# Delta-rule encoder layer: inverse merges in chunk order, and whole stationaries for the learned tokens

## Chip, core and metric

One core of a Trainium2 chip. The metric is the device time of one execution in microseconds; three executions of the kernel before took 2045.39, 2044.15 and 2043.72 us, median 2044.15. All arithmetic is in float32.

## What is computed

One layer of a bidirectional encoder on 1024 tokens, ahead of which 16 learned tokens are put. The part that matters here is the gated delta rule of branch A, for 8 heads in both directions. Cut from the reference (the kernel uses its own chunk size, 128):

```python
kk = jnp.einsum("bnhid,bnhjd->bnhij", k, k)
lmat = jnp.where(strict, beta[..., :, None] * kk * decay, 0.0)
a = lmat + jnp.eye(CHUNK, dtype=lmat.dtype)
rhs = jnp.concatenate([v * beta[..., None], k * (beta * jnp.exp(g))[..., None]], axis=-1)
sol = lax.linalg.triangular_solve(a, rhs, left_side=True, lower=True, unit_diagonal=True)
u, w = sol[..., :dv], sol[..., dv:]
...
def step(S, inp):
    v_new = u_c - jnp.einsum("bhcd,bhde->bhce", w_c, S)
    o_c = (jnp.einsum("bhcd,bhde->bhce", qd_c, S)
           + jnp.einsum("bhij,bhje->bhie", qk_c, v_new))
    S = S * gl_c[..., None, None] + jnp.einsum("bhcd,bhce->bhde", kd_c, v_new)
```

Around it: RMSNorm and one input projection (1024 to 9248 columns), short convolutions, branch B, a merge with gates, and a SwiGLU of width 2816.

## The kernel before

**Stages.** After the norm of the input (up to about 60 us) comes the stage of the input projection, whose end in the trace lies near 1060 us; then branch outputs, merge and SwiGLU, which the change does not touch. In the projection stage each unit of 128 columns is a run of three-fold matmuls (L293, L294, L295: high by high, high by low, low by high halves of a split float32), in groups of 320 to 512 tokens.

**Order of the work.** Nothing is scheduled by the hardware or by a library there: the kernel is written as generators, one for each step of a head (`g_decay`, `g_norm`, `g_inv`, `g_scan`), and a planner with a clock of its own for each engine (`T`) runs them. After every projection step the planner lets those generators go on whose due time has come; each `yield` hands back the next due time, worked out from estimates such as `pe(215)` (add 215 ns to TensorE's clock). So the numbers in `pe(...)` decide between which projection matmuls a head's step stands in TensorE's queue. VectorE's long jobs, convolution (L316 to L324) and the forward substitution (L448, L452), are fed in by `pump` from the same clocks.

**The inverse of a head.** The 1024 tokens are 8 chunks of 128 (`NC = 8`). For each chunk and direction the inverse of a triangular 128x128 matrix is needed (`NP`). `g_inv` makes the inverses of the four 32x32 blocks on the diagonal by forward substitution, which go through DRAM, and then merges: 32 to 64, and 64 to 128. `B(b)` is partitions or columns 32b to 32b+31.

- First merge, product 1 (L661 to L663): for each of four pairs (direction d, blocks a and b) and each chunk, one matmul with a 32x32 stationary `NP[B(a), c, d, B(b)]` and 32 moving columns of an inverse block (in `X64` or `Xe`), into `pt[B(b), c]`. That is 32 matmuls; all results lie in one PSUM bank. A 32x32 matmul uses a corner of the array: its rows are set by the partitions of its operands (a), its columns by those of its result (b).
- ScalarE negates the result into `T2` (L666).
- Product 2 (L670 to L674): the same four pairs and 8 chunks, into `pp[B(a), c]` with stationary `T2` (L672), and for the two pairs with `X64` also the transposed product into `px[B(b), c]` (L674): 48 matmuls, in two banks.
- Six copies, on ScalarE and VectorE by turns, put the results into `NP` and `X64` (L677 to L685); then the second merge with 64x64 blocks (L691 to L704) goes on, whose two matmuls for a chunk already stand behind one another.

In the trace a float32 matmul is two records (a transpose is one), and the stationary's load is a row of its own (PEld).

**The learned tokens.** The 16 learned tokens are a short ninth chunk (index 8). Its keys: a transpose with a 128x16 stationary (L515, a record of the helper's line L83) and k by k (L516). Its inverse, `Pm`, a 16x16 tile, is made on GpSimd and comes by DMA (L633 to L635). In the scan: the transpose of vT (L724), then L738 (stationary `Pm`, 16x16), L741 on VectorE, L743 (stationary 16x128 of the keys `kn`), whose result is the first state S0 of the forward direction.

## Time and profile before

| what | value |
|---|---|
| median of three executions | 2044.15 us |
| span of the profiled execution | 2041.3 us |
| TensorE busy in it | 2003.0 us (98%) |
| VectorE, ScalarE, GpSimd busy | 1412.3, 790.9, 109.1 us |
| L663 records in all | 512 (64 for each head) |
| L672 and L674 records in all | 512 and 256 |
| L738 and L743 records in all | 16 and 16 |

The span runs from the first instruction to the last; what an execution takes beyond it lies around it and is not in the profile. A row of the timeline has a start, a length, the engine, the line in the program, the operation, "result<-operands", the shapes (for TensorE rows x columns of the stationary, then the moving shape) and a count where rows of one kind were put together; in brackets the idle time before it and who ended that. A matmul's length is its way through the array; matmuls overlap, so what a step costs is read from start to start.

### The profile page before, as it was taken

Reading aid. Unit: us, or ns where it says so; the run is one execution under the profiler, and the core shown is the slowest. Engines: PE = TensorE matmul, PEld = TensorE weight load, DVE = VectorE, ACT = ScalarE, POOL = GpSimd, SP = SyncE. Lnnn points to the kernel's source line nnn. Section 1 sums busy time; section 2 is a strip of 40 time slices with the busy share of each in tenths; the row PEclk is TensorE's granted clock in tenths of the full one; section 3 lists DMA queues with packets and bytes.
Section 4 is the critical chain, followed back from the end, with each engine's and each line's share of the span. In section 5 each row is a group of like instructions: output and inputs, shape, how many; then the busy total and the mean of one; then the engine's idle time right before and its main releaser. Section 6 shows DMA issues by size and latency. Waiting matters only on the chain.

```text
span 2041.3 us, 32116 instructions
## 1 busy us (share of the span) xinstructions
PE 2003.0 (98%) x12075; PEld 1745.0 (85%) x12075; DVE 1412.3 (69%) x3129; ACT 790.9 (39%) x1873; POOL 109.1 (5%) x392
## 2 busy tenths in 40 slices
PE   6999999999999999999999999999999999999998
PEld 6999899999999898978888888888888888888886
DVE  6789486887977686856445534458978778756576
ACT  5363235454544554453334211124323223224343
POOL 0002110202020020201000000000000000000000
PEclk9999999999999999999999999999999999999999
DMA  4122312222222213132326734122766355487654
GB/s 140 42 85 68 74 59 62 79 63 58 73 58 81 81 58 94 57 89 78 97 70 200 255 114 142 53 83 93 238 226 221 125 180 168 153 277 247 195 176 155
DMA packets 250722, 248.40 MB, mean 122 GB/s; under 512 B 46084, under 2 KB 190773, under 8 KB 248133
## 3 DMA queue, kind: packets, MB, share of 16 engines
q1 hardware_dynamic: 250565, 246.34, 38.6%
q8 instruction: 95, 1.56, 0.3%
q14 instruction: 62, 0.51, 0.1%
HBM read 179.62 MB, written 66.67 MB: 121 GB/s over the span
## 4 chain that ended last, share of the span: by engine, by line
PE 81%; DVE 11%; ACT 3%; DMA 1%; issue 1%; SPq 0%; ACTq 0%; DVEq 0%
PE pm L293 9%; PE pm L295 9%; PE pm L294 9%; PE pm L1335 3%; PE pm L1334 3%; PE pm L1333 3%; PE pd L1334 2%; PE pd L1335 2%; PE pd L1333 2%; DVE kq L316 2%; PE pe L1335 2%; PE pe L1334 2%; PE pe L1333 2%; PE pd L771 1%; PE pd L119 1%; PE pd L121 1%
## 5 line engine op out<-in xcount | busy, mean ns | idle before, releaser
L293 PE MATMUL pm<-hTh,wh 128*128 128x512 f32 (+4 forms) x1424 | 525.8, 369 | 2.0 <-ACT wh L896 1.0
L295 PE MATMUL pm<-hTh,wl 128*128 128x512 f32 (+4 forms) x1424 | 490.1, 344 | 0.2
L294 PE MATMUL pm<-al,wh 128*128 128x512 f32 (+4 forms) x1424 | 488.9, 343 | 0.3 <-DVE al L998 0.3
L293 PEld LDWEIGHTS pm<-hTh,wh 128*128 128x128 f32 x1424 | 268.4, 189 | 21.7 <-issue 2.7
L295 PEld LDWEIGHTS pm<-hTh,wl 128*128 128x128 f32 x1424 | 267.4, 188 | 20.9 <-DVE wl L893 1.2
L294 PEld LDWEIGHTS pm<-al,wh 128*128 128x128 f32 x1424 | 268.7, 189 | 15.4 <-DVE al L998 0.7
L87 DVE TENSOR_TENSOR al<-raw,ring_h 128x1024 fp32r<-128x1024 f32 x73 | 88.3, 1222 | 64.7 <-ACT ring_h L86 64.3
L893 DVE TENSOR_TENSOR wl<-raw,wh 128x512 fp32r<-128x512 f32 x134 | 90.5, 686 | 50.8 <-ACT wh L896 50.2
L86 ACT CAST ring_h<-raw 128x1024 fp32r<-128x1024 f32 x73 | 76.7, 1055 | 105.7 <-PE pe L1478 34.8
L316 DVE SCALAR_TENSOR_TENSOR kq<-ra,wc,kq 128x520 f32<-128x520 f32 x128 | 97.4, 761 | 5.3 <-ACT kq L346 3.9
L86 ACT CAST wh<-raw 128x1024 fp32r<-128x1024 f32 x45 | 47.4, 1053 | 123.0 <-issue 29.9
L896 ACT CAST wh<-raw 128x512 fp32r<-128x512 f32 x134 | 78.8, 618 | 9.7 <-PE pm L294 9.6
L778 ACT ACTIVATE w<-pd,small 128x128 f32<-128x128 f32 x128 | 40.0, 365 | 105.0 <-PE pd L771 85.7
L452 DVE TENSOR_TENSOR fP<-fP,tm 128x135 f32<-128x135 f32 (+23 forms) x248 | 72.2, 291 | 4.9
L448 DVE TENSOR_TENSOR tm<-fP,fN 128x135 f32<-128x135 f32 (+23 forms) x248 | 72.2, 291 | 4.2
L1337 DVE TENSOR_TENSOR b<-pm,b 128x512 f32<-128x512 f32 x67 | 45.1, 686 | 33.5 <-PE pm L1335 31.1
L800 DVE SCALAR_TENSOR_TENSOR S<-S,eGl,pd 128x128 f32<-128x128 f32 x104 | 31.8, 344 | 46.6 <-PE pd L788 29.4
L87 DVE TENSOR_TENSOR wl<-raw,wh 128x1024 fp32r<-128x1024 f32 x45 | 54.9, 1219 | 9.2 <-ACT wh L86 9.1
L617 POOL TENSOR_TENSOR tm<-mP,mN 1x15 f32<-1x15 f32 (+7 forms) x120 | 42.2, 352 | 274.2 <-DMA mN<-ndm 265.7
L1337 DVE TENSOR_TENSOR b<-pd,b 128x512 f32<-128x512 f32 x54 | 36.5, 686 | 22.2 <-PE pd L1335 22.2
L316 DVE SCALAR_TENSOR_TENSOR vT<-ra,wc,vT 128x520 f32<-128x520 f32 x64 | 48.3, 755 | 2.6 <-ACT vT L346 1.1
L486 ACT ACTIVATE PQ<-PQ,negG 128x128 f32<-128x128 f32 x128 | 43.2, 394 | 15.7 <-DVE PQ L481 15.6
(623 smaller groups left out, 4649.3 us busy)
## 6 DMA issues: line engine op xcount, KB each, us to landing
raw<-in_w_in_dram SPq DMA_DIRECT2D x72, 512.0 KB
raw<-in_w_gate_up_dram SPq DMA_DIRECT2D x44, 512.0 KB
sums<-in_w_down_dram SPq DMA_DIRECT2D x22, 512.0 KB
t_d<-sums SPq DMA_DIRECT2D x11, 1024.0 KB
raw<-s_d SPq DMA_DIRECT2D x44, 256.0 KB
raw<-t_d SPq DMA_DIRECT2D x44, 256.0 KB
act_d<-b SPq DMA_DIRECT2D x43, 256.0 KB
raw<-act_d SPq DMA_DIRECT2D x33, 256.0 KB
```

The costliest lines, as they stand in the source:

```text
L86: nc.scalar.copy(hi, src)
L87: nc.vector.tensor_tensor(out=lo, in0=src, in1=hi.bitcast(F32), op=ALU.subtract)
L293: mm(po[:, :n], wh[:, k], xh[:, k, t0:t0 + n], start=(k == 0), stop=False)
L294: mm(po[:, :n], wh[:, k], xl[k][:, t0:t0 + n], start=False, stop=False)
L295: mm(po[:, :n], wl[:, k], xh[:, k, t0:t0 + n], start=False, stop=(k == KT - 1))
L316: nc.vector.scalar_tensor_tensor(out=acc, in0=raw[:, h0 + t:h0 + t + hn], scalar=wc[:, t, col:col + 1], in1=acc, op0=ALU.mult, op1=ALU.add)
L893: nc.vector.tensor_tensor(out=u[1][1][:, k], in0=u[2][:, k], in1=u[1][0][:, k].bitcast(F32), op=ALU.subtract)
L896: nc.scalar.copy(u[1][0][:, k], u[2][:, k])
L1333: mm(po, ah[:, k], bhk, start=k == 0, stop=False)
L1334: mm(po, ah[:, k], blk, start=False, stop=False)
L1335: mm(po, al[:, k], bhk, start=False, stop=k == 3)
L1337: add = lambda out, a, b: nc.vector.tensor_tensor(out=out, in0=a, in1=b, op=ALU.add)
```

## The change

Three things are done.

1. Both products of the first merge are issued with the chunk as the outer loop and the four pairs behind one another, where the pair was the outer loop. The same 32 and 48 matmuls are there.
2. The learned tokens' chunk gets whole stationaries of 128x128: the keys' transpose and k by k take columns 0 to 127 (the 16 learned tokens and the next 112), the transpose of vT too; `Pm` becomes one of two tiles of 128x128 that are set to zero once on GpSimd and receive the 16x16 inverse in their corner, so that the other rows come out as zero; L738, L741 and L743 run over all 128 partitions.
3. The planner's estimates for these steps are set anew: 1150 for 4 x 300, 1600 for 4 x 450, 330 for 120.

```diff
@@ g_norm
-        transpose(pt[:META, :P], kT[:, 0:META])
-        mm(pt[:META, P:P + META], kT[:, 0:META], kT[:, 0:META], start=True, stop=True)
-        t = pe(120)
+        transpose(pt[:, :P], kT[:, 0:P])
+        mm(pt[:, P:P + META], kT[:, 0:P], kT[:, 0:META], start=True, stop=True)
+        t = pe(330)
...
-        nc.scalar.copy(kn[:META, 8], pt[:META, :P])
+        nc.scalar.copy(kn[:, 8], pt[:, :P])
@@ g_inv
-        Pm = dn.tile([META, META], F32, tag="Pm", name=uid("Pm"), bufs=2)
-        st_["Pm"] = Pm
-        nc.sync.dma_start(Pm, pdm)
+        Pm = st_["Pm"] = meta_inv[h % 2]
+        nc.sync.dma_start(Pm[:META, :META], pdm)
...
-        for d, a, b, Xs, xo in pairs:
-            for c in range(NC):
+        for c in range(NC):
+            for d, a, b, Xs, xo in pairs:
                 mm(pt[B(b), c], NP[B(a), c, d, B(b)], Xs[B(a), c, xo:xo + 32], start=True, stop=True)
-            pe(300)
-        yield T["pe"] + HOP
+        yield pe(1150)
...
-        for d, a, b, Xs, xo in pairs:
-            for c in range(NC):
+        for c in range(NC):
+            for d, a, b, Xs, xo in pairs:
                 mm(pp[B(a), c], T2[B(b), c], NP[B(b), c, d, B(b)], start=True, stop=True)
                 if Xs is X64:
                     mm(px[B(b), c], NP[B(b), c, d, B(b)], T2[B(b), c], start=True, stop=True)
-            pe(450)
-        yield T["pe"] + HOP
+        yield pe(1600)
@@ g_scan
-                if c == 8:
-                    transpose(pt[:META, i], vT[:, 0:META])
-                else:
-                    transpose(pt[:, i], vT[:, cs(c)])
+                transpose(pt[:, i], vT[:, 0:P] if c == 8 else vT[:, cs(c)])
...
-                p = META if c == 8 else P
-                nc.scalar.activation(vS[:p, c], pt[:p, i], AF.Copy, scale=sk[:p, c:c + 1])
+                nc.scalar.activation(vS[:, c], pt[:, i], AF.Copy, scale=sk[:, c:c + 1])
...
-        mm(bank[:META, 0], Pm, vS[:META, 8], start=True, stop=True)
+        mm(bank[:, 0], Pm, vS[:, 8], start=True, stop=True)
...
-        nc.vector.tensor_scalar(out=w[:META], in0=bank[:META, 0], scalar1=ce[:META, 8, 0:1], scalar2=None, op0=ALU.mult)
+        nc.vector.tensor_scalar(out=w, in0=bank[:, 0], scalar1=ce[:, 8, 0:1], scalar2=None, op0=ALU.mult)
...
-        mm(bank[:, 1], kn[:META, 8], w[:META], start=True, stop=True)
+        mm(bank[:, 1], kn[:, 8], w, start=True, stop=True)
@@ after the pool dn is opened
+    meta_inv = [dn.tile([P, P], F32, name=f"meta_inv{i}") for i in range(2)]
+    for m_ in meta_inv:
+        nc.gpsimd.memset(m_, 0.0)
```

How the instructions stand now. First TensorE's queue at product 1 of the first head (XT holds `X64`; a row is one call, x8 means eight alike), before:

```order
L295 MATMUL pm_2500<-hTh,wl_2393 128x322
L663 MATMUL pd_2524<-XT_2438,NP_1485 32x32 x8
L663 MATMUL pd_2524<-Xe_2437,NP_1485 32x32 x16
L663 MATMUL pd_2524<-XT_2438,NP_1485 32x32 x8
L293 MATMUL pm_2500<-hTh,wh_2392 128x322
```

and in the changed kernel (its line 662 is line 663 of before), the first five of its rows there:

```order
L295 MATMUL pm_2503<-hTh,wl_2397 128x322
L662 MATMUL pd_2527<-XT_2441,NP_1489 32x32
L662 MATMUL pd_2527<-Xe_2440,NP_1489 32x32 x2
L662 MATMUL pd_2527<-XT_2441,NP_1489 32x32 x2
L662 MATMUL pd_2527<-Xe_2440,NP_1489 32x32 x2
```

Eight matmuls on one corner followed one another before; now the corner changes with every matmul, and the four of a chunk are XT, Xe, Xe, XT.

Second, product 2 of the same head on TensorE (T is `T2`; line 672 of before is 670 now, 674 is 672), where before the pair with both results passes to the two pairs with one:

```order
L674 MATMUL pd_2570<-T_315_2523,NP_1485 32x32
L672 MATMUL pd_2569<-NP_1485,T_315_2523 32x32
L674 MATMUL pd_2570<-T_315_2523,NP_1485 32x32
L672 MATMUL pd_2569<-NP_1485,T_315_2523 32x32 x17
L674 MATMUL pd_2570<-T_315_2523,NP_1485 32x32
```

and now, the first chunk and the start of the second:

```order
L670 MATMUL pd_2572<-NP_1489,T_314_2526 32x32
L672 MATMUL pd_2573<-T_314_2526,NP_1489 32x32
L670 MATMUL pd_2572<-NP_1489,T_314_2526 32x32 x3
L672 MATMUL pd_2573<-T_314_2526,NP_1489 32x32
L670 MATMUL pd_2572<-NP_1489,T_314_2526 32x32
```

Each chunk now has all six of its matmuls behind one another.

Third, the start of the last head's scan on TensorE, from the last transposes of vT to the small matmul with the learned tokens' inverse, before:

```order
L83 MATMUL pd_12118<-ident,vT_9608 128x128 x3
L293 MATMUL pm_12083<-hTh,wh_11851 128x512
L294 MATMUL pm_12083<-al_122,wh_11851 128x512
L295 MATMUL pm_12083<-hTh,wl_11852 128x512
L293 MATMUL pm_12083<-hTh,wh_11851 128x512
L294 MATMUL pm_12083<-al_123,wh_11851 128x512
L295 MATMUL pm_12083<-hTh,wl_11852 128x512
L738 MATMUL pd_12133<-vS_12095,Pm_11839 16x128
```

and now (line 731):

```order
L83 MATMUL pd_12087<-ident,vT_9445 128x128 x3
L293 MATMUL pm_12034<-hTh,wh_11853 128x512
L294 MATMUL pm_12034<-al_123,wh_11853 128x512
L295 MATMUL pm_12034<-hTh,wl_11854 128x512
L731 MATMUL pd_12097<-vS_12066,meta_inv_657 128x128
```

The matmul's result has 128 rows where it had 16, and one projection step stands in between where there were two: the planner's changed clock has moved the step by one place.

## The prediction

> **What bounds the kernel now.** I read the windows by stage first, then the chain of waits, then TensorE's timeline at each place that the change touches. The change lies in the stage from 110 to 1060 us (projections with the delta rule's steps strewn in). Three windows, whose columns are the window, its length, busy time (x instructions) of PE, PEld, DVE, ACT, POOL, granted clock, DMA share and GB/s:

> ```profile
> 110.00:1060.00 950.00, 943.95 (x7150) 856.60 (x7149) 688.94 (x1956) 432.51 (x1365) 102.70 (x356) 1.00 0.26 73
> 110.00:200.00 90.00, 89.64 (x546) 85.68 (x545) 79.92 (x201) 45.91 (x160) 12.28 (x47) 1.00 0.28 80
> 1000.00:1060.00 60.00, 60.00 (x462) 50.25 (x461) 18.56 (x48) 22.80 (x64) 0.00 (x0) 1.00 0.23 67
> ```

> TensorE is idle for 6.05 of these 950 us, at full clock; the last window, with the last head's steps, has no idle TensorE at all, so no tail of waits hangs behind the last scan. VectorE has 261 us to spare over the stage, but at its start, up to 200 us, it is 89% busy. The chain that ended last says the same, and warns that VectorE is near:

> ```profile
> PE 81%; DVE 11%; ACT 3%; DMA 1%; issue 1%; SPq 0%; ACTq 0%; DVEq 0%
> ```

> So time that a step takes on TensorE's queue is time of the kernel, as long as the other engines keep up.

> **The change part by part.** Product 1 of the merge (L663) has 32 calls for each head; each call is two records in the trace, so 64 records. The first head's, columns start, length, engine, line, operation, count:

> ```profile
> 228.15 0.59 PE L663 MATMUL pd<-XT,NP 32*32 32x32 f32 x13
> 228.56 0.21 PE L663 MATMUL pd<-Xe,NP 32*32 32x32 f32 x1
> 228.59 0.19 PE L663 MATMUL pd<-XT,NP 32*32 32x32 f32 x1
> 228.61 0.19 PE L663 MATMUL pd<-Xe,NP 32*32 32x32 f32 x1
> ...
> 228.68 0.88 PE L663 MATMUL pd<-Xe,NP 32*32 32x32 f32 x26
> ...
> 229.49 0.57 PE L663 MATMUL pd<-XT,NP 32*32 32x32 f32 x13
> ```

> Read the last row first: 13 records of one pair in 0.57 us, the last of them 0.19 long, so twelve steps in 0.38 us: 0.0317 us from record to record as long as one pair stays on its own 32x32 corner of the array. Now the rows at 228.56: there the second pair (Xe) already runs while the first (XT) still ends, each at its own pace of about 0.03 us, and neither is slowed by the other. The first record starts at 228.15, the last at 229.49 + 0.57 - 0.19 = 229.87: 1.72 us, of which only these few overlaps at the three borders were saved. The new order puts the four pairs behind one another for each chunk, and all four lie on different corners (rows and columns 0,1; 2,3; 1,0; 3,2). If each keeps its pace, the stretch is that of one pair: 15 steps of 0.0317 = 0.48, with 0.02 for a slower first step and about 0.02 for the shifts between four starts, 0.52 us. Gain 1.20 us.

> Product 2 (L672 and L674, 48 calls, 96 records) already has places with two and with three corners at work:

> ```profile
> 231.53 0.21 PE L672 MATMUL pd<-NP,T 32*32 32x32 f32 x1
> 231.54 0.21 PE L674 MATMUL pd<-T,NP 32*32 32x32 f32 x1
> ...
> 231.99 0.19 PE L672 MATMUL pd<-NP,T 32*32 32x32 f32 x2
> 232.00 0.19 PE L674 MATMUL pd<-T,NP 32*32 32x32 f32 x1
> 232.03 0.19 PE L672 MATMUL pd<-NP,T 32*32 32x32 f32 x2
> 232.03 0.19 PE L674 MATMUL pd<-T,NP 32*32 32x32 f32 x1
> ...
> 233.26 0.19 PE L674 MATMUL pd<-T,NP 32*32 32x32 f32 x1
> ```

> At 231.99 to 232.03 three corners start a record each, and the next three follow about 0.03 us later: three cost what one does. (L672 and L674 of one pair share their rows of the array, so shared rows are no hindrance either.) The stretch is 231.53 to 233.26, 1.73 us. The new order has six corners in each chunk. With one pace for all it would be 0.52; but there are twelve records in each chunk, and neighbouring starts lie between 0.005 us (three from 231.99 to 232.00) and 0.01 us (231.53, 231.54) apart. I take 0.0065, nearer to the row with three corners: 8 x 12 x 0.0065 = 0.62 us; gain 1.11 us. Bounds for both products: at best the whole pace, 1.20 and 1.21; at worst what two corners show, 0.0317 / 2 for each record, which makes 1.01 and 1.52 us and a gain of 0.71 + 0.21.

> [...]

> Now the learned tokens. Two calls in the scan have stationaries of 16 rows (L738 also 16 columns); beside them a place with four records of full stationaries:

> ```profile
> 244.29 0.34 PE L294 MATMUL pm<-al,wh 128*128 128x384 f32 x1
> 244.46 0.34 PE L295 MATMUL pm<-hTh,wl 128*128 128x384 f32 x1
> 244.73 0.39 PE L738 MATMUL pd<-vS,Pm 16*16 16x128 f32 x2
> ...
> 245.39 0.40 PE L294 MATMUL pm<-al,wh 128*128 128x512 f32 x1
> ...
> 246.08 0.39 PE L294 MATMUL pm<-al,wh 128*128 128x512 f32 x1
> 246.31 0.39 PE L295 MATMUL pm<-hTh,wl 128*128 128x512 f32 x1
> 246.63 0.48 PE L743 MATMUL pd<-w,kn 16*128 16x128 f32 x2
> ...
> 247.38 0.40 PE L294 MATMUL pm<-al,wh 128*128 128x512 f32 x1
> ...
> 257.25 0.39 PE L295 MATMUL pm<-hTh,wl 128*128 128x512 f32 x1
> 257.48 0.61 PE L771 MATMUL pd<-r,NP 128*128 128x128 f32 x4
> ...
> 258.16 0.39 PE L294 MATMUL pm<-al,wh 128*128 128x512 f32 x1
> ```

> From the L295 ahead to the second projection matmul behind, less the steps of the two projections in between (0.17 for 384 columns, 0.23 for 512, both from start to start here): L738 costs 0.93 - 0.17 - 0.23 = 0.53 us, L743 1.07 - 0.46 = 0.61, and four full records 0.91 - 0.46 = 0.45, so two of them 0.22. The small shapes lose their time in front and behind, where the array passes from the full shape to the small one and back. With full stationaries L738 gains 0.31 and L743 0.39: 0.70 us for each head.

> The learned tokens' keys (L515 and L516, ahead of four full transposes):

> ```profile
> 116.10 0.31 PE L294 MATMUL pm<-al,wh 128*128 128x320 f32 x1
> 116.24 0.31 PE L295 MATMUL pm<-hTh,wl 128*128 128x320 f32 x1
> 116.39 0.27 PE L83 MATMUL pe<-ident,kq 128*16 128x128 f32 x1
> 116.59 0.21 PE L516 MATMUL pe<-kq 128*16 128x16 f32 x2
> 116.74 0.66 PE L83 MATMUL pe<-ident,kq 128*128 128x128 f32 x4
> ...
> 117.38 0.31 PE L294 MATMUL pm<-al,wh 128*128 128x320 f32 x1
> ```

> That is 1.14 - 2 x 0.15 = 0.84 us for seven records. Full stationaries with few moving columns are seen in the gates, where two records step by 0.23 although only 72 columns move:

> ```profile
> 100.78 0.39 PE L1120 MATMUL pe<-gc,Ub 128*128 128x72 f32 x2
> 101.01 0.39 PE L1120 MATMUL pe<-gc,Eb 128*128 128x72 f32 x2
> ```

> Seven records of 0.11 are 0.77: gain 0.07 us. Were L516's records as short as half of that, it would be 0.18; I keep 0.07. The short transpose of vT among two full ones I set at nothing: it moves the same 128 columns either way, and the short transpose at 116.39 starts one ordinary step of 0.15 behind its projection, so there is no gap to win in front of a transpose. The wider copies on ScalarE and VectorE (L520, L730, L741) cover 128 partitions with as many elements in each, so they cost what they did. The DMA of the inverse into the larger tile keeps its size and its place on SyncE's queue. The two memsets on GpSimd add a wait: they stand in its queue until the start-up tiles whose memory they take are free, and behind them stand the small memsets of the convolution's rows (L343), for which ScalarE's copies of the projections and the convolution wait.

> ```profile
> 68.82 0.10 POOL L343 MEMSET ra<- 128x2 f32 x1 [62.74 <-DVE kq L316]
> ```

> The first of those had itself to wait for VectorE until 68.82, after 62.74 us without work, so the new wait is covered if the start-up tiles are free by then; the price is nothing, or once a few microseconds in the convolutions.

> Sum for each head: 1.20 + 1.11 + 0.70 + 0.07 = 3.08 us, for eight heads 24.6 us, all on TensorE's queue.

> What is late next: the copies behind product 2.

> ```profile
> 233.48 0.36 ACT L682 COPY NP<-pd 32x256 f32<-32x256 f32 x1 [3.00 <-PE pd L674]
> ...
> 235.64 0.36 ACT L685 COPY XT<-pd 32x256 f32<-32x256 f32 x1 [0.94 <-DVE XT L684]
> ```

> They already begin when the last record of product 2 has ended (233.26 + 0.19), not pair by pair, so the new order takes nothing from them; they hand on to each other until 236.00, 2.7 us after that last record started, and the second half of the next merge waits for them where fewer projections lie between. The planner's counts have moved a little, so some heads have a projection step less there: I allow 0.8 us in all. VectorE gets 3 us less for each head in a stage where it has 261 to spare, and I allow 1.5 us for places where it is just in time. 24.6 - 2.3 = 22.3 us.

> The profiled execution's span is 2041.3 us, 2.85 under the median of 2044.15; the loss of 22.3 from the span goes one to one into the time: 2041.3 - 22.3 = 2019.0 us of span, and 2021.9 us.

> **The rivals.** Two at a time: the array or its queue serves no more than two corners in one pace. For it: the steady stretches in product 2 are of two; three are seen only over a few records. Gain (0.71 + 0.21 + 0.77) x 8 = 13.5 us, less 1 given back: 2031.6 us.

> One bank: pairs that write the same PSUM bank from different rows exclude each other as soon as they alternate, and the overlaps seen at the borders are an exception. Without overlap product 1 is 64 x 0.0317 = 2.03 us and the 64 records of L672 too, 0.31 and 0.30 worse than now; 0.77 - 0.61 = 0.16 us for each head remains, 1.3 us in all: 2042.9 us. Against it stand the rows at 228.56 and 232.03. [...]

> Slower: VectorE becomes the bound. The planner's costs are changed, so heads' steps are placed earlier among the projections, and TensorE comes sooner to results that VectorE has still to make. Its place is the key products, which wait already:

> ```profile
> PE pe L542 <- DVE PQ L571: 2.9, 5, 0.9
> ```

> (2.9 us in five waits, longest 0.9.) It decides once the waits grow by more than the 24.6 us won, over 3 us for each head, as if every one of the 64 L542 calls came some 0.45 us too early and not five of them. With 29 us of it the time is 2048.6. Against it: VectorE is 73% busy over the stage, and the 89% lie ahead of the first merge, where only the keys' 0.07 us are won; and the amount of projection work between the steps of a head is about the same in both orders.

> **How the numbers follow.** Forecast 0.70, between 2018 and 2027; two at a time 0.15, 2029 to 2034; VectorE taking back half of the gain 0.04, 2027 to 2040; one bank 0.07, 2040 to 2044; slower 0.04. The predicted time is the forecast's, 2021.9. At its lower end all records keep the pace (0.8 us more), L516 is shorter (0.9) and nothing is given back (2.3): 2017.9; I set 2017. The upper end takes in two at a time: 2034. A measurement of this kernel can tell 0.2%, 4.1 us, from no change. Faster by more than that: 0.70 + 0.15 + 0.04 and 0.02 of one bank, 0.91; within: 0.05; slower: 0.04.

> **What would show it.** In the changed kernel's timeline product 1 should take about 0.5 us from first to last start and product 2 about 0.6; 1.0 and 1.5 would be the rival with two; 2.0 each the bank. The scan's two small calls should stand as 128*128 with some 0.22 us of cost. TensorE's idle time from 110 us on should stay under 10 us, with L542 and the second merge at the head of what waits; 30 us there would be the slower rival. The forecast is wrong if the stretches are short and the time is still above 2034.

## The result and the profile after

The changed kernel takes 2034.13 us (median of four executions, 2032.91 to 2035.01), the kernel before 2044.77 us (2043.72 to 2046.32): a ratio of 0.9946 with a 95% interval of 0.9934 to 0.9959. It is 10.6 us faster where 22.3 were forecast, and lies just above the range's upper end, 2034. The profiled execution's span went from 2041.3 to 2031.6 us.

Two windows of the changed kernel (the columns as before), the first of them the one that the prediction began with:

```profile
110.00:1060.00 950.00, 934.81 (x7217) 853.41 (x7217) 696.88 (x1980) 439.01 (x1386) 101.20 (x356) 1.00 0.27 74
300.00:400.00 100.00, 95.82 (x802) 89.33 (x801) 73.68 (x206) 45.66 (x154) 11.79 (x44) 0.98 0.23 62
```

In the same 950 us TensorE now gets through 7217 matmul records instead of 7150, so it is further along; but it is idle for 15.2 us instead of 6.05. Of these, 4.2 us lie in one stretch of 100 us, where the clock's mean is also under 1. The chain that ended last has kept its shape:

```profile
PE 80%; DVE 11%; ACT 3%; DMA 2%; issue 1%; SPq 0%; POOL 0%; DVEq 0%; ACTq 0%; POOLq 0%
```

**The steps that were changed.** First the merge of the first head: the first and the last rows of product 1 and of product 2.

```profile
228.62 0.21 PE L662 MATMUL pd<-XT,NP 32*32 32x32 f32 x1
228.63 0.22 PE L662 MATMUL pd<-Xe,NP 32*32 32x32 f32 x2
...
229.18 0.19 PE L662 MATMUL pd<-XT,NP 32*32 32x32 f32 x1
...
230.84 0.21 PE L670 MATMUL pd<-NP,T 32*32 32x32 f32 x1
230.84 0.21 PE L672 MATMUL pd<-T,NP 32*32 32x32 f32 x1
...
231.66 0.19 PE L672 MATMUL pd<-T,NP 32*32 32x32 f32 x1
```

From first to last start product 1 takes 0.56 us (1.72 before) and product 2 0.83 (1.73 before). Divided by 63 and by 95 steps both give nearly the same, 8.9 and 8.7 ns from record to record, although one has four corners at work and the other six.

Then the first of the scan's two small calls, among projections.

```profile
242.87 0.34 PE L295 MATMUL pm<-hTh,wl 128*128 128x384 f32 x1
243.04 0.38 PE L731 MATMUL pd<-vS,meta_inv 128*128 128x128 f32 x2
243.18 0.48 PE L293 MATMUL pm<-hTh,wh 128*128 128x512 f32 x1
243.50 0.40 PE L294 MATMUL pm<-al,wh 128*128 128x512 f32 x1
```

By the prediction's own reckoning (from the projection ahead to the second one behind, less two projection steps) L731 costs 0.63 - 0.17 - 0.23 = 0.23 us; it was 0.53.

**Where the time stayed.** What TensorE waits for between 110 and 1100 us in the changed kernel (us in all, times, longest):

```profile
PE pe L542 <- DVE PQ L571: 5.1, 4, 3.3
PE pd L689 <- DVE XT L681: 2.8, 2, 2.6
PE pe L83 <- DVE Nm L525: 2.1, 2, 1.2
PE pm L293 <- issue: 1.3, 1, 1.3
PE pd L672 <- issue: 1.3, 1, 1.3
```

Four idle times of more than 1.2 us stand out; in the kernel before the longest of this stretch was 0.9. (The row of L83 stands there too, with the same 2.1 us in all.) I take the four one by one.

The longest is at 331 us. TensorE's rows, then VectorE's:

```profile
329.55 0.70 PE L542 MATMUL pe<-kq 128*128 128x256 f32 x2
...
330.81 0.31 PE L295 MATMUL pm<-hTh,wl 128*128 128x320 f32 x1
334.46 0.67 PE L542 MATMUL pe<-kq 128*128 128x256 f32 x2 [3.34 <-DVE PQ L571]
```

```profile
329.21 3.21 DVE L316 SCALAR_TENSOR_TENSOR vT<-ra,wc,vT 128x520 f32<-128x520 f32 x4
332.33 0.17 DVE L548 TENSOR_SCALAR small<-small 128x9 f32<-128x9 f32 x1
...
333.25 0.61 DVE L567 SCALAR_TENSOR_TENSOR NP<-pe,small,PQ 128x128 f32<-128x128 f32 x2
333.89 0.42 DVE L571 TENSOR_TENSOR PQ<-pe,PQ 128x256 f32<-128x256 f32 x1
```

A key product (L542) needs a PSUM tile that VectorE frees with L571. VectorE works without a gap, but on four taps of a convolution that stand ahead in its queue; the head's small steps (L548 to L571) come behind them. VectorE is not later than in the kernel before, whose rows for the same taps and the same L571 are

```profile
331.28 3.21 DVE L316 SCALAR_TENSOR_TENSOR vT<-ra,wc,vT 128x520 f32<-128x520 f32 x4
...
337.66 0.42 DVE L571 TENSOR_TENSOR PQ<-pe,PQ 128x256 f32<-128x256 f32 x1
```

and for TensorE's same two key products

```profile
333.82 0.70 PE L542 MATMUL pe<-kq 128*128 128x256 f32 x2
338.23 0.67 PE L542 MATMUL pe<-kq 128*128 128x256 f32 x2 [0.69 <-DVE PQ L571]
```

It is 3.8 us earlier, but TensorE is earlier still. From one key product to the next it now has 1.6 us of work (329.55 to 334.46, less the wait of 3.34) where it had 3.7 (333.82 to 338.23, less the wait of 0.69).

The wait costs more than itself. Windows behind it (TensorE's granted clock is the third figure from the end):

```profile
335.00:336.00 1.00, 1.00 (x20) 0.94 (x21) 1.00 (x4) 1.00 (x3) 0.00 (x0) 0.60 0.03 8
336.00:338.00 2.00, 2.00 (x22) 1.88 (x21) 1.03 (x3) 1.16 (x4) 0.00 (x0) 0.50 0.00 0
338.00:340.00 2.00, 2.00 (x13) 2.00 (x12) 1.94 (x6) 0.60 (x2) 0.00 (x0) 0.85 0.00 0
```

Soon after the idle time the clock is halved for about 3.4 us (0.50 is granted from 335.19 to 338.61 us), which is a loss of 0.4 + 1.0 + 0.3 = 1.7 us.

The second long idle time is at 667 us, where the second merge (L689) waits for a copy of the first merge's results on VectorE (L681, 669.80 us). The copies run by turns on two engines, and ScalarE's first one (L679) stood behind other work:

```profile
666.98 0.64 ACT L321 ACTIVATE rb<-vT 128x520 f32<-128x520 f32 x1 [0.72 <-DVE vT L316]
667.53 0.68 ACT L486 ACTIVATE PQ<-PQ,negG 128x128 f32<-128x128 f32 x2
668.11 0.34 ACT L679 COPY NP<-pd 32x256 f32<-32x256 f32 x1
```

Product 2 had ended at 665.1, so its first copy started 3 us late: ScalarE stood until VectorE's taps had let L321 go, and then had L486, a step of a head, to do as well.

The third and the fourth have no releaser ("issue"):

```profile
785.19 0.30 PE L293 MATMUL pm<-hTh,wh 128*128 128x320 f32 x1 [1.26 <-issue]
...
987.43 0.22 PE L672 MATMUL pd<-T,NP 32*32 32x32 f32 x2 [1.26 <-issue]
```

The second of these stands inside product 2, two records before its end, where nothing is waited for. The profile's row on the queue that brings instructions gives the hint:

```profile
q8 instruction: 95, 1.56, 0.3%
```

95 packets of 16 KB on an instruction queue, for 12075 matmuls and 12075 weight loads: one packet for 254 records. In the trace such a packet starts at 782.78 and at 985.02 us, and both idle times end 2.4 us after it. So TensorE seems to have used up its instructions before the next block (what one such packet brings) was there.

**The account.** From 110 us to the start of the last projection matmul I summed the work on TensorE: the projections at their steady pace, and each step of a head at what it costs where nothing holds it up. What is left of that stretch I call lost time (waits, half-clock windows, fetches). Before, the stretch ends at 1091.4 us (so the stage of the projections ends there, and not near 1060 us), with 12.7 us lost; after, at 1080.6, with 24.3. The heads' steps became 22.8 us cheaper (257.4 to 234.6 us), and 11.6 us more are lost: 22.8 - 11.6 = 11.2 us, against 10.6 in the times. Of the 11.6, the four idle times with the half clock are 3.3 + 1.7 + 2.6 + 1.3 + 1.3 = 10.2. (A rougher reading agrees: between 110 and 1060 us the idle time grew by 9.1 us, and the half clock took 1.7.)

### The profile page after: what moved, and what is told of

The parts are those of the page before. It is cut to its first block, busy times and chain, and to the rows that moved or that the text cites. A ratio compares the mean times of both kernels' runs of the same rounds, so it can differ in the third digit from the quotient of the medians.

```text
span 2031.6 us, 32113 instructions
## 1 busy us (share of the span) xinstructions
PE 1982.7 (98%) x12075; PEld 1732.7 (85%) x12075; DVE 1412.6 (70%) x3129; ACT 791.9 (39%) x1873; POOL 108.0 (5%) x394
## 4 chain that ended last, share of the span: by engine, by line
PE 80%; DVE 11%; ACT 3%; DMA 2%; issue 1%; SPq 0%; POOL 0%; DVEq 0%; ACTq 0%; POOLq 0%
PE pm L293 9%; PE pm L295 9%; PE pm L294 9%; PE pm L1330 3%; PE pm L1331 3%; PE pm L1329 3%; PE pd L1330 2%; PE pd L1331 2%; PE pd L1329 2%; DVE kq L316 2%; PE pe L1331 2%; PE pe L1330 2%; PE pe L1329 2%; PE pd L121 1%; PE pd L120 1%
## 5 line engine op out<-in xcount | busy, mean ns | idle before, releaser
L293 PE MATMUL pm<-hTh,wh 128*128 128x384 f32 (+4 forms) x1424 | 525.9, 369 | 3.5 <-issue 1.3
L295 PE MATMUL pm<-hTh,wl 128*128 128x384 f32 (+4 forms) x1424 | 490.4, 344 | 0.4 <-issue 0.2
L294 PE MATMUL pm<-al,wh 128*128 128x384 f32 (+4 forms) x1424 | 488.8, 343 | 0.3 <-DVE al L991 0.3
L295 PEld LDWEIGHTS pm<-hTh,wl 128*128 128x128 f32 x1424 | 267.6, 188 | 20.6 <-issue 0.5
L294 PEld LDWEIGHTS pm<-al,wh 128*128 128x128 f32 x1424 | 269.0, 189 | 17.1 <-issue 1.4
L316 DVE SCALAR_TENSOR_TENSOR kq<-ra,wc,kq 128x520 f32<-128x520 f32 x128 | 97.3, 760 | 3.8 <-ACT kq L346 2.4
L771 ACT ACTIVATE w<-pd,small 128x128 f32<-128x128 f32 x128 | 40.1, 365 | 111.0 <-PE pd L764 102.7
L1333 DVE TENSOR_TENSOR b<-pd,b 128x512 f32<-128x512 f32 x54 | 36.5, 686 | 22.3 <-PE pd L1331 22.3
L486 ACT ACTIVATE PQ<-PQ,negG 128x128 f32<-128x128 f32 x128 | 43.4, 393 | 15.6 <-DVE PQ L481 15.5
L316 DVE SCALAR_TENSOR_TENSOR vT<-ra,wc,vT 128x520 f32<-128x520 f32 x64 | 48.2, 753 | 1.7 <-ACT vT L346 0.6
```

The lines of the kernel that those rows point to most:

```text
L293: mm(po[:, :n], wh[:, k], xh[:, k, t0:t0 + n], start=(k == 0), stop=False)
L294: mm(po[:, :n], wh[:, k], xl[k][:, t0:t0 + n], start=False, stop=False)
L295: mm(po[:, :n], wl[:, k], xh[:, k, t0:t0 + n], start=False, stop=(k == KT - 1))
L316: nc.vector.scalar_tensor_tensor(out=acc, in0=raw[:, h0 + t:h0 + t + hn], scalar=wc[:, t, col:col + 1], in1=acc, op0=ALU.mult, op1=ALU.add)
L1333: add = lambda out, a, b: nc.vector.tensor_tensor(out=out, in0=a, in1=b, op=ALU.add)
```

## The experiments

Two theories stood first. "Order": the new estimates of the planner put the heads' steps at worse places, whatever the merges cost. "Slack": the old merges had given VectorE time, which the shorter merges take away in any order. In each row below the estimates are those for product 1, product 2 and the keys; lost time is reckoned as above, with the part that is half clock in brackets.

**The old estimates with the new matmuls**

```diff
-        t = pe(330)
+        t = pe(120)
...
-        yield pe(1150)
+        yield pe(1200)
...
-        yield pe(1600)
+        yield pe(1800)
```

> The changed kernel, its matmuls and tiles as they are, with the planner's three estimates put back to those of before, so that every engine's instructions stand in the order of before. In the two traces at hand the steps touched cost TensorE 22.8 us less (257.4 to 234.6 us of work that is not projection, from 110 us to the end of the stage), and its waits there grew from 12.7 to 24.3 us. Theory order: the waits come from the new places of the heads' steps, which happen to meet VectorE late at a few of them; then this kernel's waits are 12 to 16 us and its time 22 us under before, about 2022 to 2024. Rival slack: TensorE simply became faster than the planner's clock, and VectorE is late in any order; then the waits are 20 to 25 us here too and the time is about 2032 to 2035.

Measured: 2027.22 us, ratio 0.9918 (0.9904 to 0.9931); lost time 17.0 us (1.7), no idle time of the issue kind. Both are between what the two theories expected.

**The new estimates with the old matmuls**

```diff
-            pe(300)
-        yield T["pe"] + HOP
+        yield pe(1150)
...
-            pe(450)
-        yield T["pe"] + HOP
+        yield pe(1600)
...
-        t = pe(120)
+        t = pe(330)
```

> The kernel before with nothing but the planner's three estimates of the changed kernel (1150, 1600, 330): the instructions stand in the changed kernel's order, but merges and learned tokens cost TensorE what they did. Theory order: the waits come along, 18 to 24 us of them, and the time is 5 to 11 us above before, 2050 to 2056. Rival slack: the slow merges leave VectorE its time, waits 11 to 15 us, time within 3 us of before.

Measured: 2047.02 us, ratio 1.0016 (1.0007 to 1.0025); lost time 14.5 us. So the order alone adds 1.8 us of lost time to the old matmuls, and the faster matmuls alone add 4.3 to the old order, 1.7 of them half clock. Both together add 11.6. Neither theory gives that alone.

**The estimates set to what was measured**

```diff
-        t = pe(330)
+        t = pe(290)
...
-        yield pe(1150)
+        yield pe(880)
...
-        yield pe(1600)
+        yield pe(1150)
```

> The changed kernel with the planner's estimates set to what its trace shows: 880 for product 1, 1150 for product 2, 290 for the keys. Rival slack: the planner gives VectorE the time that it really has, waits 12 to 16 us, time about 2022 to 2025. Theory order: this is just another order, waits anywhere from 12 to 25 us and no reason to be at the low end; 2022 to 2036.

Measured: 2024.04 us, ratio 0.99 (0.9887 to 0.9914); lost time 14.7 us, with one idle time of 1.4 us of the issue kind, again inside product 2:

```profile
776.23 0.21 PE L672 MATMUL pd<-T,NP 32*32 32x32 f32 x1 [1.36 <-issue]
```

**Each part of the change alone**, with the old estimates: first the merges,

```diff
-        for d, a, b, Xs, xo in pairs:
-            for c in range(NC):
+        for c in range(NC):
+            for d, a, b, Xs, xo in pairs:
```

> The kernel before with the first merge's two products in chunk order and nothing else: order and planner's estimates of before, learned tokens with small stationaries. By the traces the merges save (2.033 - 0.88 + 2.045 - 1.148) x 8 = 16.4 us of TensorE's time. Theory order: waits stay at 12 to 15 us, time about 2028 to 2030. Rival slack: waits grow to 18 to 22 us, time about 2034 to 2038.

then the learned tokens' whole stationaries.

```diff
-        mm(bank[:META, 0], Pm, vS[:META, 8], start=True, stop=True)
+        mm(bank[:, 0], Pm, vS[:, 8], start=True, stop=True)
...
-        mm(bank[:, 1], kn[:META, 8], w[:META], start=True, stop=True)
+        mm(bank[:, 1], kn[:, 8], w, start=True, stop=True)
```

> The kernel before with nothing but the whole stationaries for the learned tokens, in the order of before and with its planner's estimates. By the traces L738 saves 0.295, L743 0.38 and the keys 0.12 us for each head, 6.4 us in all. If the parts add up (with the merges alone 11.7 us and both together in the old order 16.7 us under before), this is 4 to 7 us under before, about 2037 to 2040, with waits of 12 to 15 us.

Measured: the merges 2032.23 us, ratio 0.994 (0.9928 to 0.9953), with 16.4 us less work and 3.5 more lost (16.2), again between what the two theories expected; the tokens 2038.4 us, ratio 0.9967 (0.9954 to 0.998), with 6.4 us less work and none more lost (12.7). The whole stationaries, 128*128 calls where the small shape stood, bring all that they save; the merges are where time is given back.

**The keys' estimate alone**

```diff
-        t = pe(330)
+        t = pe(120)
```

> The changed kernel with the keys' estimate alone put back from 330 to 120; 1150 and 1600 for the merges stay. The order is then close to that of before. Theory order: the waits fall to 15 to 18 us, time 2025 to 2029. Rival slack (the merges' estimates, 0.7 us over the truth for each head, make VectorE late): waits stay at 20 to 25 us, time 2031 to 2035.

Measured: 2025.4 us, ratio 0.9909 (0.9894 to 0.9924); lost time 15.6 us. One number that adds or takes away no work is worth 8.7 us here (4.3 of them are the half clock and the idle times of the issue kind, which this kernel does not have in the stage).

**Less work on VectorE** (the kernel leaves out one tap of a convolution)

```diff
+                if t < 4:
-                nc.vector.scalar_tensor_tensor(out=acc, in0=raw[:, h0 + t:h0 + t + hn], scalar=wc[:, t, col:col + 1],
+                    nc.vector.scalar_tensor_tensor(out=acc, in0=raw[:, h0 + t:h0 + t + hn], scalar=wc[:, t, col:col + 1],
```

> The changed kernel, its order and estimates untouched, without one of the four further taps of the convolution of q, k and v (the last one is left out: 48 instructions of 0.76 us less on VectorE, and q, k and v come out wrong). If the waits that came with the change are TensorE's waits for VectorE, they fall by 6 to 12 us and the time comes to 2022 to 2028. If they come from elsewhere (ScalarE, instruction fetch, the tiles' buffers), they stay above 20 us and the time above 2031. The two stretches of 1.3 us in which TensorE waits for nothing that the profile shows stay in both cases, or move.

Measured: 2017.6 us, ratio 0.9879 (0.9858 to 0.9901); lost time 14.0 us, with the order on TensorE and ScalarE unchanged. (The time is below what was expected in part because the kernel also gains some 4 us ahead of 110 us, 3.1 of them idle time of TensorE between 60 and 110 us; the lost time leaves that out.) What remains of the long waits:

```profile
PE pe L543 <- DVE PQ L572: 2.6, 2, 2.4
PE pd L690 <- DVE XT L682: 1.8, 1, 1.8
PE pd L673 <- issue: 1.0, 1, 1.0
```

The longest two (one line lower here) shrink, from 3.3 and 2.6 to 2.4 and 1.8, so they are waits for VectorE; the idle time inside product 2 stays, so it is not.

**Estimates between the new ones and the true ones**

```diff
-        t = pe(330)
+        t = pe(300)
...
-        yield pe(1150)
+        yield pe(1000)
...
-        yield pe(1600)
+        yield pe(1350)
```

> The changed kernel with estimates between its own and the true ones: 1000, 1350 and 300 (own 1150, 1600, 330; true 880, 1150, 290). Rival slack: waits between the two, 16 to 21 us, time 2026 to 2031. Theory order: a further draw, waits 13 to 25 us, and no reason to lie between.

Measured: 2018.08 us, ratio 0.9871 (0.9856 to 0.9886); lost time 9.8 us. This ended the theory of slack, which expected 16 to 21: the same fast merges, and TensorE waits less than in the kernel before. It is also below the 13 to 25 that the theory of order allowed.

**Instruction fetch**: 64 records more near 12 us, with their weight loads 128 of the 254 for which one packet comes, to shift the borders of all later blocks.

```diff
+                for _ in range(32):
+                    mm(pt[:32, :32], ident[:32, :32], ident[:32, :32], start=True, stop=True)
                 transpose(pt[:, :120], rows[:120, 0], 120)
```

> The changed kernel with 32 calls of a 32x32 matmul (64 records) more in TensorE's queue ahead of the transpose of the convolution's weights near 12 us, where TensorE then waits 5.5 us for VectorE; the tile they write is written again by that transpose. All else keeps its order on every engine. Theory 'instruction fetch': the two idle times of about 1.3 us that the profile calls issue, inside product 2 of the first merge near 986 us and behind L295 near 783.6, come because a burst of short records uses up the fetched instructions faster than the next block arrives; 64 records move every later block border by half a block, so both vanish at these two places (2.6 us less waiting; others may appear where the border now falls into a burst), and the waits for VectorE (4.5 us near 331 to 334, 3.0 near 667) stay. Time 2031 to 2035. Theory 'something else at that place' (a result, a bank, a semaphore that the profile doesn't show): both idle times stay where they are to within a record.

Measured: 2034.73 us, ratio 0.9952 (0.9935 to 0.9969). The waits of its trace, the first two and the one of the issue kind:

```profile
PE pe L542 <- DVE PQ L571: 5.5, 5, 3.2
PE pd L689 <- DVE XT L681: 2.6, 1, 2.6
...
PE pd L670 <- issue: 0.3, 1, 0.3
```

Both idle times of 1.3 us are gone, and the waits for VectorE are where they were: as the theory of fetches has it. What this saves is not seen in the time. Leaving out the end of the program, the profile has five half-clock windows of 3.4 us where the changed kernel's has one, two of them behind the wait of 2.6 us at the second merge, behind which that one kept its full clock, one behind the longest wait, and two ahead of 110 us; the three in the stage, 5.1 us, hide the gain (lost time 24.1 us, 19.0 without them, against 22.6 without its one in the changed kernel). The mean granted clock of its four executions, 0.994 to 0.996 against 0.995 to 0.997, says that half clock was more frequent in them too. What decides on such a window is in the last section; here the wait of 2.6 us fell otherwise between the borders that are described there.

**Two neighbours of the middle estimates**

```diff
-        yield pe(1150)
+        yield pe(1000)
...
-        yield pe(1600)
+        yield pe(1350)
```

> The changed kernel with the planner's 1000 and 1350 for the merge's products and the changed kernel's 330 for the keys (the middle clock had 1000, 1350 and 300). The order on TensorE differs from the middle clock's in 48 places. Theory 'each set of estimates draws an order': waits from 110 us to the stage's end anywhere between 10 and 24 us, time 2018 to 2034. Theory 'the keys' 330 makes the waits': 20 us or more, time 2030 to 2034. Theory 'the merge's estimates make them': 8 to 12 us, time 2018 to 2021.

```diff
-        t = pe(330)
+        t = pe(300)
...
-        yield pe(1150)
+        yield pe(950)
...
-        yield pe(1600)
+        yield pe(1250)
```

> The changed kernel with 950, 1250 and 300, a step from the middle clock (1000, 1350, 300) towards the durations measured; the order differs from the middle clock's in 8 places on TensorE and 2 on VectorE. Theory 'each set of estimates draws an order': so near an order gives nearly the same waits, 8 to 12 us, but for those 8 places, and a time of 2016 to 2022. If it is 4 us or more away, a few places decide.

Measured: 2022.46 us, ratio 0.9891 (0.9876 to 0.9905), lost time 12.5 us, 1.3 of it once more an idle time inside product 2; and 2018.57 us, ratio 0.9871 (0.9856 to 0.9886), lost time 10.1 us. The keys' 330 in place of 120, beside the estimates 1150 and 1600, cost 8.7 us; 330 in place of 300, beside 1000 and 1350, costs 2.7 us of lost time and 4.4 in the gain. The first of these two kernels came out just beyond what was expected if the merges' estimates make the waits, and far from what was expected if the keys' 330 makes them; the second came out as expected.

**Estimates below the truth**

```diff
-        t = pe(330)
+        t = pe(290)
...
-        yield pe(1150)
+        yield pe(600)
...
-        yield pe(1600)
+        yield pe(850)
```

> The changed kernel with the merge's products priced far below what they take, 600 and 850 (measured: 880 and 1148 ns with the passage between shapes), keys 290. So far, with the products priced 0.7 to 1.0 us too high together for a head, the waits from 110 us to the stage's end were 15.6 to 24.3 us; priced up to 0.35 us too high, 9.8 to 12.5; priced true 14.7, of which 1.5 is one idle time of instruction fetch. Theory 'an estimate that is too high puts TensorE's clock ahead, and the heads' steps come before VectorE': priced 0.58 us too low, the waits are few, 8 to 13 us without idle times of the issue kind, time 2016 to 2021. Theory 'any mismatch costs': 16 to 24 us, time 2024 to 2033. Theory 'each set of estimates draws an order': anywhere from 10 to 24, and the waits stand at places that none of the other kernels has.

Measured: 2017.66 us, ratio 0.9872 (0.9855 to 0.9888), the lowest time of all kernels with the whole computation and 16 us below the changed kernel; lost time 8.7 us. (Against the kernel before, run beside it, it gains 26.4 us, the middle estimates 26.8 and their lesser neighbour 26.3: these three are equal within the noise.) TensorE's waits are down to these:

```profile
PE pe L83 <- DVE Nm L525: 1.3, 2, 1.0
PE pe L542 <- DVE PQ L571: 0.6, 1, 0.6
```

At the place where the changed kernel waited 3.3 us, VectorE's row and TensorE's now read:

```profile
336.41 0.41 DVE L571 TENSOR_TENSOR PQ<-pe,PQ 128x256 f32<-128x256 f32 x1
```

```profile
333.84 0.70 PE L542 MATMUL pe<-kq 128*128 128x256 f32 x2
337.85 0.60 PE L542 MATMUL pe<-kq 128*128 128x256 f32 x2
```

VectorE frees the tile 2.5 us later than in the changed kernel, and nobody waits: from one key product to the next TensorE now has 4.0 us of work, not 1.6. "Any mismatch costs" is refuted; an estimate that is too low did no harm.

All of them beside one another. "Too high" is the sum of the two estimates for the products less what they take (0.88 + 1.15 us, or 2.03 + 2.05 in the old order of their matmuls); "account" is the work saved (22.8, 16.4, 6.4 or 0 us) less the lost time added to the 12.7 of before; "measured" the difference of the medians.

| kernel | estimates | too high, us | lost, us (half clock) | account, us | measured, us |
|---|---|---|---|---|---|
| low | 600, 850, 290 | -0.58 | 8.7 | 26.8 | 26.4 |
| true | 880, 1150, 290 | 0.00 | 14.7 | 20.8 | 19.9 |
| less than middle | 950, 1250, 300 | 0.17 | 10.1 | 25.4 | 26.3 |
| middle | 1000, 1350, 300 | 0.32 | 9.8 | 25.7 | 26.8 |
| middle, keys 330 | 1000, 1350, 330 | 0.32 | 12.5 | 23.0 | 22.4 |
| keys 120 | 1150, 1600, 120 | 0.72 | 15.6 | 19.9 | 19.5 |
| **the change** | 1150, 1600, 330 | 0.72 | 24.3 (1.7) | 11.2 | 10.6 |
| old estimates | 1200, 1800, 120 | 0.97 | 17.0 (1.7) | 18.5 | 16.7 |
| merges alone | 1200, 1800, 120 | 0.97 | 16.2 | 12.9 | 11.7 |
| tokens alone | 1200, 1800, 120 | -1.08 | 12.7 | 6.4 | 6.5 |
| new estimates alone | 1150, 1600, 330 | -1.33 | 14.5 | -1.8 | -3.1 |

The account gives each time to within 1.8 us, so nothing large is missing from it. With the products 0.72 us or more too high, 15.6 to 24.3 us are lost; at 0.32 or less, with the fast merges, 8.7 to 14.7. How an estimate does this was only argued: every step of a head is put into TensorE's queue when TensorE's own count has reached the time at which another engine's result is due; where that count runs ahead of the chip, fewer projections stand in front of the step. What the runs show is that the count matters, and that with the fast merges more is lost where it is high; the two groups nearly touch, at 14.7 and 15.6 us, and the low side rests on one kernel. At the key product near 331 us alone TensorE waits not at all with the low estimates, then 0.77 us (true), 0.98, 1.17 and 1.57 (the three in the middle), 2.28 (old) and 3.34 (the change), nearly in the order of the sum; the keys' 120, with 0.86, are out of line. The runs do not show a law: true estimates lose more than their neighbours on both sides, and the 8.7 us between 330 and 120 for the keys beside 1150 and 1600 stay unexplained by the sum of the two products. A small shift of an estimate moves steps at some places by one projection, and single places such as the one at 331 us decide.

## Why the prediction was wrong

**The local gains held.** Product 1 costs 0.88 us with its passages in front and behind, 2.03 before: 1.15 won (1.20 forecast). Product 2: 2.05 to 1.15, 0.90 won (1.11). L738: 0.52 to 0.22, 0.30 won (0.31). L743: 0.61 to 0.23, 0.38 won (0.39). Keys: 0.84 to 0.72, 0.12 won (0.07). In all 2.85 us for each head, 22.8 us instead of 24.6; the 1.8 us are nearly all product 2. I had taken 0.0065 us between neighbouring starts, from a spot with three corners at work; it is 0.0087, and with 96 records the count of records and no longer the pace of a corner sets the stretch.

**What was set at nothing was nothing.** The transpose of vT costs 0.33 us before and after. The wider copies take nearly what they took: 0.266 us for the keys on ScalarE (0.254 before, median of eight) and 0.351 for `w` on VectorE (0.339 before). The memsets waited as described, and were done in time:

```profile
60.18 0.35 POOL L1148 MEMSET meta_inv<- 128x128 f32 x2 [54.08 <-PE pe L1010]
69.19 0.10 POOL L343 MEMSET ra<- 128x2 f32 x1 [8.66 <-DVE kq L316]
```

The convolution's memset still waits for VectorE as the last, until 69.19 us (68.82 before).

**The step that failed is the one on what is late next.** "VectorE gets 3 us less for each head in a stage where it has 261 to spare, and I allow 1.5 us for places where it is just in time", and 0.8 for the copies: 2.3 us in all, and 11.6 more than before were lost. The two places are those named there (key products behind L571, second merge behind the copies), but not their size. The 261 us are a mean over a stage of 950 us; at 331 us VectorE has four taps, 3.2 us, ahead of the head's steps, and slack elsewhere is of no use to them. The trace of before already showed a wait for VectorE at this place, the 0.69 us above. Two shares come on top that no step of the prediction had: 1.7 us of half clock behind the wait, and 2.6 us of what looks like instruction fetch. Of the 11.1 us between the forecast gain of 22.3 and the 11.2 of the account, 9.3 are lost in this step and 1.8 in the local gains.

**The rivals.** What happened comes nearest to the one in which VectorE takes back half of the gain, between 2027 and 2040 us (of the 10.2 us above, 5.9 are waits for VectorE and 1.7 the half clock behind one); with a chance of 0.04 it had far too little. The slower rival described the mechanism (heads' steps earlier among the projections, TensorE too soon at the key products) but needed it at every key product; the waits came at few. I held that "the amount of projection work between the steps of a head is about the same in both orders"; at the place that cost most it fell from 3.7 us to 1.6. "Two at a time" has a time close to the one measured, 2031.6 us, and is still wrong: product 1 takes 0.56 us, not 1.01. "One bank" is out: the records of four corners that write one bank follow each other at 8.9 ns, where without overlap it would be the 31.7 ns of one corner and 2.0 us for product 1. This is measured with each corner writing partitions of its own in the bank, and for no other case.

**The prediction's own test** went against it: the stretches are short and the time is above 2034, though only by 0.1 us, less than the 2.1 us between the four executions. The idle time is 15 us, above the 10 of the forecast and below the 30 of the slower rival.

## What to carry to other kernels

Where an order is planned from estimated durations, a faster step has two effects: its own gain, and a new order, whose waits can take much of it back (22.8 us won and 11.6 lost here); so after such a change try several estimates before judging it; here those below the truth or just above it did best, and the true ones lost some 6 us against them. Slack of another engine is read at the place where it is needed, from what stands ahead in its queue, not as a mean of the stage; a short wait that is there already warns that time won ahead of it can be lost in it. Here idle times of TensorE of 1.90, 2.6 and 3.3 us were followed by half clock, at a cost of another 1.7 us; those of 1.90 and 2.6 us were so in one kernel and not in another, so it is in part luck, as the next section shows.

## What was not expected of the hardware

```profile
97.93 0.41 PE L1113 MATMUL pe<-gc,U2f 128*128 128x72 f32 x2 [1.90 <-DVE gc L1107]
95.96:99.37 3.41, 1.51 (x12) 1.47 (x12) 2.32 (x6) 3.10 (x7) 0.13 (x2) 1.00 0.00 0
99.37:102.79 3.42, 3.42 (x14) 3.38 (x13) 3.14 (x6) 1.64 (x7) 0.00 (x0) 0.50 0.54 153
```

```profile
96.57 0.41 PE L1113 MATMUL pe<-gc,U2f 128*128 128x72 f32 x2 [1.90 <-DVE gc L1107]
92.20:95.61 3.41, 2.47 (x15) 2.15 (x13) 2.47 (x5) 0.69 (x2) 0.13 (x2) 1.00 0.00 0
95.61:99.02 3.41, 2.45 (x17) 2.48 (x18) 3.07 (x8) 2.51 (x7) 0.00 (x0) 1.00 0.00 0
```

  In the first the whole wait lies between two borders, and TensorE is busy for 1.51 of the 3.41 us; in the second a border, at 95.61, parts the wait, and it is busy for 2.47 and 2.45. Between 60 and 1995 us of the 14 traces there are ten slots of the grid in which TensorE is busy for less than half; nine of them are followed by half clock. Of the others, more than 7900, only two are, and one of these two is itself at half clock. The exception among the ten is the wait of 2.6 us in the changed kernel, with 1.52 us busy from 666.28 to 669.69; in the kernel with the shifted blocks the slot of the same wait has 1.14, and half clock follows. It is no sharp rule: near 48 us five traces go to half clock behind a slot with 2.3 us busy. Each such window of 3.41 us at 0.50 costs 1.7 us, which by itself spreads the times of one kernel.
- A burst of 96 short records that reaches the border of an instruction block seems to leave TensorE without instructions for 1.0 to 1.4 us, in the changed kernel until 2.4 us after a block's transfer starts; the evidence is this timing and the shift of the blocks, which took both away. Of the eleven kernels with the new order of the merge four show it, in or shortly behind product 2; of the three with the old order none.
